# VectorE 32x32 blocks and spread SBUF-to-SBUF transfers in place of some TensorE transposes in a one-layer hybrid decoder

## Chip, core and metric

One core of one Trainium2 chip runs the whole program. The metric is the device time of one execution in microseconds (us), lower is better. The engines are called PE (TensorE; PEld is its weight load), DVE (VectorE), ACT (ScalarE), POOL (GpSimd) and SP (SyncE, which here only issues transfers).

## What is computed

One decoder layer on 256 tokens of width 2048 in float32, and a final norm. Cut to what matters:

```python
h = rms_norm(x); z = h @ w_in                  # 2048 -> 10240
qa, ka, va, qb, kb, vb, ga, gb = split_columns(z)
oa = differential_attention(rope(qa), rope(ka), va)    # 8 heads
ob = stick_breaking_attention(qb, kb, vb)              # 8 heads
m  = sigmoid(ga) * (oa @ w_proj_a) + sigmoid(gb) * (ob @ w_proj_b)
x  = x + m @ w_out
x  = x + memory_cross_attention(rms_norm(x), rms_norm(mem))
u  = rms_norm(x) @ w_up                        # 2048 -> 11264
u  = causal_depthwise_conv(u)                  # width 3, along the tokens
x  = x + (silu(u[:, :5632]) * u[:, 5632:]) @ w_down
return rms_norm(x)
```

## The kernel before

Every matrix product is cut into units of 512 output columns. `product` (L177) keeps two PSUM tiles of 128 tokens x 512 columns for a unit and walks over the contraction in 128-row blocks. Weights arrive by SP in 1 MB pieces (four 128-row blocks, tile `raw`, three buffers). `split_w` (L160) divides each half of a piece, 128 x 1024 values, into a high part on ACT (L162) and a low part on DVE (L163), in three buffers each; `mm3` (L166) then issues three matmuls per block and token half: high x high (L168), low x high (L169), high x low (L170). A unit over 2048 rows is four pieces, eight halves and 96 matmuls of 512 columns.

Products need the activations with the features on the partitions, while a unit's result has the tokens there. So results are transposed in 128 x 128 squares on PE, against an identity, into PSUM: `transposed` (L113, matmul L134) for the merge `mT`, the residuals `x1T`, `x2T` and the cross-attention inputs; `proj_T` (L243, matmul L258) for the queries and keys of both attentions; `gated` (L555, matmul L562) for each of the 22 units of the up projection. One unit is 8 squares. The copy out of PSUM is ACT and DVE work (L117, L118, L122, L123, L260), or the convolution itself, whose ACT (L568) and DVE instructions (L570, L572) read the transposed PSUM tile.

This side work is written as generators. `spawn(gen, delay)` starts one after so many halves, `tick` runs after each half of a product and lets the due ones go on; a `yield n` asks for n more halves. A scheduler then fixes the order of each engine's instructions, apart from SP's, which keeps the order of the program text. An SP instruction that must wait holds up all later transfers, the weights among them.

The up projection's loop (L585) evacuates both PSUM tiles of a unit to `zu` with the scale `r2` (L588) and spawns `gated` two halves later. The SBUF tiles that live long (`x2T`, `xr`, `gT`, queries, keys, gates) share one pool of 34 buffers, `b4`.

Of the kernel before, what the change touches and what calls it, by code (L numbers as in the profile page):

```python
# [17 lines left out]
S = 256          # tokens  # L18
NT = S // P      # token blocks
D = 2048  # L20
KD = D // P      # 128-row blocks of the model width
FF = 5632
KF = FF // P
U = 512          # columns of one product unit
KB = 4           # 128-row blocks per weight transfer
# [6 lines left out]
# columns of the packed per-partition parameters  # L32
# [13 lines left out]
def hybrid_layer(ctx: ExitStack, tc: tile.TileContext, x, xT, mem, memT, gmix, par, gfin,  # L46
# [28 lines left out]
    # additive masks of the diagonal blocks: [q, k] -> 0 where k <= q (k < q), else NEG  # L75
# [8 lines left out]
    # Work that is emitted between the products: generators that yield the number of  # L84
    # half blocks of weights to let pass before they go on.
# [6 lines left out]
    def tick(most=2):  # L92
        clock[0] += 1
        for t in [t for t in tasks if t[0] <= clock[0]][:most]:
            try:
                t[0] = clock[0] + next(t[1])
            except StopIteration:
                tasks.remove(t)
# [14 lines left out]
    def split(dst, src, gains=None):  # L113
        """dst[:, 0] + dst[:, 1] = src, or src * gain, in two parts of 12 bits.
        dst [P, 2, 2, S], src [P, 2, S]; gains: a [P, 1] column per 128-row block."""
# [10 lines left out]

    def transposed(dst, src, n, name, gains=None):
        """dst: act tiles of the 4 row blocks n*4.. of the transpose; src [P, NT, U]."""
# [11 lines left out]

    def sumsq(dst, src):
        junk = wk.tile([P, U], F32, tag="w2", name="junk")
        nc.scalar.activation(out=junk[:, :src.shape[-1]], in_=src, func=AF.Square, accum_out=dst)

    def rstd(ss, n, width, name):
        """(sum over the last axis of ss [P, n, m] / width + EPS) ** -0.5 -> [P, n]"""
# [19 lines left out]
    def mm3(out, a, b, start=True, stop=True):  # L166
        """out (+)= (a[0] + a[1]).T @ (b[0] + b[1]) without the product of the two low parts."""
# [9 lines left out]
    def product(xs, w, u, kt_n, name, pieces=None, before=None, heap=False):  # L177
        """x @ w[:, unit u] for both token blocks -> two PSUM tiles [P, U].
        pieces: 128-row blocks per transfer; before(kt): called ahead of the transfer from kt on."""
# [25 lines left out]
    def load_split(src, gains, i, name):  # L205
        """Split act tile i of a transposed input [P, KD, S] in DRAM, scaled by gains."""
# [27 lines left out]
    def proj_T2(ps, r, name):  # L234
        """Evacuate a unit scaled by r and transpose it: act tiles of heads 0, 1 and 2, 3."""
# [7 lines left out]
    def proj_T(ps, r, name, rotate=False):  # L243
        """Evacuate a unit scaled by r and transpose it: [P (dim), 4 (head), S]."""
# [9 lines left out]
        def rest():  # L254
            for t in range(NT):
                pt = sm_tile(f"{name}_tp")
                for h in range(4):
                    nc.tensor.transpose(out=pt[:, h * P:(h + 1) * P],  # L258
                                        in_=zs[t][:, h * P:(h + 1) * P], identity=ident)
                nc.vector.tensor_copy(out=dst[:, :, t * P:(t + 1) * P],  # L260
                                      in_=pt.rearrange("p (h s) -> p h s", h=4))
            yield 0
        spawn(rest(), 2)
        return dst

    def proj_n(ps, r, name):
        """Evacuate a unit scaled by r: [P (token), NT, U]."""
# [5 lines left out]
    def attn_T(a, name):  # L273
        """Causal weights of one head [q block][P, K] -> [P (key), 3 * P]:
        keys 0 for both query blocks, then keys 1 for query block 1."""
# [8 lines left out]
    # differential attention  # L284
    oaT = [None] * 4

    def diff_head(h):
        qT, kT, v, hh = qa[h // 4], ka[h // 4], va[h // 4], h % 4
        # scores of the two maps, in a bank each: query block 0 in 0:P, query block 1 in P:3 * P
# [62 lines left out]
    # stick-breaking attention, two heads at a time  # L352
    obT = [None] * 4

    def stick_pair(g):
        aw = [[], []]
        for i in range(NT):
# [14 lines left out]
            # softplus(z) = max(z, 0) + ln(1 + exp(-|z|)), zero where masked  # L372
# [27 lines left out]
    # the input projection in units; the attention of a group of heads runs between the products  # L400
# [21 lines left out]
    # lam = exp(q1.k1) - exp(q2.k2) + LAM_INIT, negated, on all partitions  # L422
# [19 lines left out]
    for i in range(2):  # L442
# [3 lines left out]
        spawn(chain(diff_head, (4 * i, 4 * i + 2)))  # L446
        spawn(chain(diff_head, (4 * i + 1, 4 * i + 3)), 2)
    for i in range(2):
# [3 lines left out]
        spawn(chain(stick_pair, (2 * i, 2 * i + 1)))  # L452
# [3 lines left out]
    # branch projections, gated and merged  # L456
    mT = [None] * 8
    for n in range(4):
# [9 lines left out]
        spawn(transposed(mT, ga, n, f"mT{n}"), 2)  # L468
# [6 lines left out]
    # output projection and residual  # L475
# [14 lines left out]
    for n in range(4):  # L490
# [4 lines left out]
        spawn(transposed(x1T, xr[n], n, f"x1T{n}", lambda k: col("g_x", k)), 2)  # L495
# [57 lines left out]
    gT = [None] * (KF // 2)  # L553

    def gated(i, z):  # L555
        us = []
        for part in range(2):          # gate, value
            pt = sm_tile("uT").rearrange("p (j s) -> p j s", j=2)
            for j in range(2):
                for t in range(NT):  # L560
                    c = (2 * part + j) * P
# [22 lines left out]
    for i in range(KF // 2):  # L584
        ps = product(x2T, w_up, i, KD, f"up{i}")  # L585
        z = [wk.tile([P, U], F32, tag="w2", name=f"zu{t}") for t in range(NT)]
        for t in range(NT):
            nc.scalar.activation(out=z[t], in_=ps[t], func=AF.Copy, scale=r2[:, t:t + 1])  # L588
# [123 lines left out]
```

## Time and profile before

| | |
|---|---|
| median of 3 runs | 1521.09 us (1521.03 to 1521.51) |
| profiled execution, from its first to its last instruction | 1518.9 us; its own time outside that span is not listed, the runs' median is 2.2 us above it |
| PE busy | 1503.4 us, 99% of the span, 6904 matmuls |
| PEld, DVE, ACT, POOL busy | 82%, 59%, 52%, 4% |
| clock that PE was granted | mean 0.998 of full speed |
| transfers | 287.78 MB, 189 GB/s, 54.5% of the 16 DMA engines' time on SP's queue |

The page gives the busy time of each engine, then the same in 40 slices of the span, then the transfers, and then the chain of work that ended last. A busy PE row is made of pipelined matmuls, so starts in the timeline say more than durations.

### The profile page before, as it was taken

The numbers are of one execution on the slowest core, as the hardware profiler recorded it, in microseconds if no ns is written. First come the engines' busy times: TensorE is split into PE (matmuls) and PEld (weight loads), VectorE is DVE, ScalarE is ACT, GpSimd is POOL, SyncE is SP. The second block draws the span as 40 slices with busy tenths as digits, with TensorE's granted clock in tenths as the row PEclk, the third lists the DMA queues.
The fourth block names the chain that finished last, engine by engine and source line by source line (L and its number), as shares of the span: only waits on it lengthen the run. The fifth ranks groups of instructions, "written<-read, shape, count | busy, mean of one in ns | idle before, by whom it ended". The sixth has DMA issues, their size and how long they took to land.

```text
span 1518.9 us, 17599 instructions
## 1 busy us (share of the span) xinstructions
PE 1503.4 (99%) x6904; PEld 1243.2 (82%) x6904; DVE 896.7 (59%) x1131; ACT 784.7 (52%) x1074; POOL 53.7 (4%) x72
## 2 busy tenths in 40 slices
PE   8999999999999999999999999999999999999997
PEld 6878788888888888888888888888888888888886
DVE  5575666564444565664666667666666666444562
ACT  6454555465555344664565555555555555344441
POOL 0202000000000010000000000000000000000010
PEclk9999999999999999999999999999999999999999
DMA  9544444445555556755355555555555555655561
GB/s 349 187 159 152 162 166 167 167 166 194 194 194 193 183 193 246 265 197 192 139 191 174 189 194 178 183 194 185 179 191 192 174 190 192 222 194 192 197 230 73
DMA packets 44003, 287.78 MB, mean 189 GB/s; under 512 B 5008, under 2 KB 5008, under 8 KB 11152
## 3 DMA queue, kind: packets, MB, share of 16 engines
q1 hardware_dynamic: 43488, 286.13, 54.5%
q8 instruction: 54, 0.88, 0.2%
q10 hardware_dynamic: 432, 0.53, 0.1%
q14 instruction: 29, 0.24, 0.0%
HBM read 284.54 MB, written 2.10 MB: 189 GB/s over the span
## 4 chain that ended last, share of the span: by engine, by line
PE 98%; issue 1%; DMA 0%; DVE 0%; ACT 0%; SPq 0%; POOLq 0%; POOL 0%; DVEq 0%
PE up_mm L170 11%; PE up_mm L169 11%; PE up_mm L168 11%; PE dn_mm L168 5%; PE dn_mm L170 5%; PE dn_mm L169 5%; PE g_mm L168 4%; PE g_mm L169 4%; PE g_mm L170 4%; PE wo_mm L170 2%; PE wo_mm L168 2%; PE wo_mm L169 2%; PE uT L562 1%; PE va_mm L169 1%; PE qb_mm L169 1%; PE qb_mm L168 1%
## 5 line engine op out<-in xcount | busy, mean ns | idle before, releaser
L163 DVE TENSOR_TENSOR up_lo<-up_raw,up_hi 128x1024 fp32r<-128x1024 f32 x176 | 215.7, 1226 | 170.3 <-ACT up_hi L162 167.8
L162 ACT CAST up_hi<-up_raw 128x1024 fp32r<-128x1024 f32 x176 | 185.5, 1054 | 197.5 <-PE up_mm L170 176.5
L170 PE MATMUL up_mm<-up_hi,x2T 128*128 128x512 f32 x704 | 274.1, 389 | 0.0
L169 PE MATMUL up_mm<-up_lo,x2T 128*128 128x512 f32 x704 | 274.0, 389 | 0.0
L168 PE MATMUL up_mm<-up_hi,x2T 128*128 128x512 f32 x704 | 254.8, 392 | 0.0
L163 DVE TENSOR_TENSOR dn_lo<-dn_raw,dn_hi 128x1024 fp32r<-128x1024 f32 x88 | 109.9, 1253 | 101.0 <-ACT dn_hi L162 95.7
L170 PEld LDWEIGHTS up_mm<-up_hi,x2T 128*128 128x128 f32 x704 | 132.2, 188 | 27.4
L169 PEld LDWEIGHTS up_mm<-up_lo,x2T 128*128 128x128 f32 x704 | 132.3, 188 | 26.7
L168 PEld LDWEIGHTS up_mm<-up_hi,x2T 128*128 128x128 f32 x704 | 132.2, 188 | 26.6
L162 ACT CAST dn_hi<-dn_raw 128x1024 fp32r<-128x1024 f32 x88 | 92.0, 1056 | 118.0 <-PE dn_mm L170 103.7
L170 PE MATMUL dn_mm<-dn_hi,gT 128*128 128x512 f32 x352 | 136.9, 389 | 0.0
L169 PE MATMUL dn_mm<-dn_lo,gT 128*128 128x512 f32 x352 | 136.9, 389 | 0.0
L163 DVE TENSOR_TENSOR g_lo<-g_raw,g_hi 128x1024 fp32r<-128x1024 f32 x64 | 78.4, 1225 | 83.8 <-ACT g_hi L162 83.8
L168 PE MATMUL dn_mm<-dn_hi,gT 128*128 128x512 f32 x352 | 126.3, 389 | 0.0
L162 ACT CAST g_hi<-g_raw 128x1024 fp32r<-128x1024 f32 x64 | 67.3, 1053 | 73.4 <-PE g_mm L170 70.2
L169 PE MATMUL g_mm<-g_lo,hT 128*128 128x512 f32 x256 | 100.0, 391 | 0.0
L170 PE MATMUL g_mm<-g_hi,hT 128*128 128x512 f32 x256 | 99.8, 390 | 0.0
L168 PE MATMUL g_mm<-g_hi,hT 128*128 128x512 f32 x256 | 90.7, 391 | 0.0
L170 PEld LDWEIGHTS dn_mm<-dn_hi,gT 128*128 128x128 f32 x352 | 66.1, 188 | 13.8
L169 PEld LDWEIGHTS dn_mm<-dn_lo,gT 128*128 128x128 f32 x352 | 66.1, 188 | 13.7
L168 PEld LDWEIGHTS dn_mm<-dn_hi,gT 128*128 128x128 f32 x352 | 66.1, 188 | 13.6
L170 PEld LDWEIGHTS g_mm<-g_hi,hT 128*128 128x128 f32 x256 | 48.1, 188 | 10.0
(301 smaller groups left out, 2664.5 us busy)
## 6 DMA issues: line engine op xcount, KB each, us to landing
up_raw<-in_w_up SPq DMA_DIRECT2D x88, 1024.0 KB, 4.9
dn_raw<-in_w_dn SPq DMA_DIRECT2D x44, 1024.0 KB, 4.9
g_raw<-in_w_in SPq DMA_DIRECT2D x32, 1024.0 KB, 5.0
wo_raw<-in_w_out SPq DMA_DIRECT2D x16, 1024.0 KB, 5.0
ka_raw<-in_w_in SPq DMA_DIRECT2D x8, 1024.0 KB, 6.1
va_raw<-in_w_in SPq DMA_DIRECT2D x8, 1024.0 KB, 5.0
qb_raw<-in_w_in SPq DMA_DIRECT2D x8, 1024.0 KB, 4.9
kb_raw<-in_w_in SPq DMA_DIRECT2D x8, 1024.0 KB, 4.9
```

What stands on the lines that cost most here:

```text
L162: nc.scalar.copy(out=hi, in_=src)
L163: nc.vector.tensor_tensor(out=lo, in0=src, in1=hi.bitcast(F32), op=ALU.subtract)
L168: nc.tensor.matmul(out, lhsT=a[0], rhs=b[0], start=start, stop=False)
L169: nc.tensor.matmul(out, lhsT=a[0], rhs=b[1], start=False, stop=False)
L170: nc.tensor.matmul(out, lhsT=a[1], rhs=b[0], start=False, stop=stop)
L562: nc.tensor.transpose(out=pt[:, j, t * P:(t + 1) * P], in_=z[t][:, c:c + P], identity=ident)
```

## The change

A new helper `turn` transposes the 32 x 32 blocks of a 128 x 512 tile on DVE; `regroup` then moves the blocks to their places with 16 SBUF-to-SBUF transfers on SP, each from 32 partitions to 32 partitions in 256 runs of 128 bytes, two transfers per half of a product. `flipped` does this for the merge units 0 and 1 and the first residual's units 0 to 2; `proj_T` does it for all eight units of queries and keys; the up projection does it for all 22 units, where ACT now scales the PSUM tiles in place. `transposed` on PE stays for the rest. Delays of the attention chains and of `gated` grow, and `tick` lets four tasks go on instead of two. Comments were removed, so line numbers shift (L162 is L195 now, L163 is L196, L562 is gone).

```diff
-    def tick(most=2):
+    def tick(most=4):
...
+    def turn(blk, src, t):
+        nc.vector.transpose(out=blk[:, :, t * P:(t + 1) * P], in_=src.rearrange("p (f c) -> p f c", c=P))
+
+    def regroup(dst, blk, per=2):
+        q = P // 4
+        d, s = (v.rearrange("p f (t c) -> p (f t) c", t=NT) for v in (dst, blk))
+        for i in range(16):
+            a, b = i // 4, i % 4
+            nc.sync.dma_start(out=d[b * q:(b + 1) * q, :, a * q:(a + 1) * q],
+                              in_=s[a * q:(a + 1) * q, :, b * q:(b + 1) * q])
+            if i % per == per - 1:
+                yield 1
+
+    def flip_tile(name):
+        return chunk_tile(f"{name}_blk", [P, U // P, S])
...
+    def flipped(dst, src, n, name, gains=None):
+        blk = flip_tile(name)
+        for t in range(NT):
+            turn(blk, src[:, t], t)
+        yield 8
+        z = chunk_tile(f"{name}_z", [P, U // P, S])
+        yield from regroup(z, blk)
+        for h in range(2):
+            k0 = 4 * n + 2 * h
+            dst[k0 // 2] = act_tile(f"{name}_{h}")
+            split(dst[k0 // 2], z[:, 2 * h:2 * h + 2], None if gains is None else [gains(k0), gains(k0 + 1)])
+        yield 0
...
         def rest():
+            blk = flip_tile(name)
             for t in range(NT):
-                pt = sm_tile(f"{name}_tp")
-                for h in range(4):
-                    nc.tensor.transpose(out=pt[:, h * P:(h + 1) * P],
-                                        in_=zs[t][:, h * P:(h + 1) * P], identity=ident)
-                nc.vector.tensor_copy(out=dst[:, :, t * P:(t + 1) * P],
-                                      in_=pt.rearrange("p (h s) -> p h s", h=4))
-            yield 0
-        spawn(rest(), 2)
+                turn(blk, zs[t], t)
+            yield 7
+            yield from regroup(dst, blk)
+        spawn(rest(), 1)
...
-        spawn(chain(diff_head, (4 * i, 4 * i + 2)))
-        spawn(chain(diff_head, (4 * i + 1, 4 * i + 3)), 2)
+        spawn(chain(diff_head, (4 * i, 4 * i + 2)), 10)
+        spawn(chain(diff_head, (4 * i + 1, 4 * i + 3)), 12)
...
-        spawn(chain(stick_pair, (2 * i, 2 * i + 1)))
+        spawn(chain(stick_pair, (2 * i, 2 * i + 1)), 10)
...
-        spawn(transposed(mT, ga, n, f"mT{n}"), 2)
+        spawn((flipped if n < 2 else transposed)(mT, ga, n, f"mT{n}"), 0 if n < 2 else 2)
...
-        spawn(transposed(x1T, xr[n], n, f"x1T{n}", lambda k: col("g_x", k)), 2)
+        spawn((flipped if n < 3 else transposed)(x1T, xr[n], n, f"x1T{n}", lambda k: col("g_x", k)), 0 if n < 3 else 2)
...
-    def gated(i, z):
+    def gated(i, blk):
+        uT = chunk_tile("uT", [P, U // P, S])
+        yield from regroup(uT, blk)
         us = []
-        for part in range(2):          # gate, value
-            pt = sm_tile("uT").rearrange("p (j s) -> p j s", j=2)
-            for j in range(2):
-                for t in range(NT):
-                    c = (2 * part + j) * P
-                    nc.tensor.transpose(out=pt[:, j, t * P:(t + 1) * P], in_=z[t][:, c:c + P],
-                                        identity=ident)
+        for part in range(2):
             u = wk.tile([P, 2, S], F32, tag="w2", name="u")
             for j in range(2):
                 f = part * KF + 2 * i + j
+                z = uT[:, 2 * part + j]
...
-        z = [wk.tile([P, U], F32, tag="w2", name=f"zu{t}") for t in range(NT)]
-        for t in range(NT):
-            nc.scalar.activation(out=z[t], in_=ps[t], func=AF.Copy, scale=r2[:, t:t + 1])
-        spawn(gated(i, z), 2)
+        blk = flip_tile(f"up{i}")
+        for t in range(NT):
+            nc.scalar.activation(out=ps[t], in_=ps[t], func=AF.Copy, scale=r2[:, t:t + 1])
+            turn(blk, ps[t], t)
+        spawn(gated(i, blk), 8)
```

What this does to the order on the engines is shown at three places. The first is SP in the middle of the up projection; `up_raw` is a weight piece, `uT` the transposed unit, `up_blk` the unit with its blocks turned, and the names in brackets are the eight completion semaphores of transfers (DMAHW0 to 7) and the engines that an issue waits for. Before:

```order
L190 DMA up_raw<-in_w_up 128x2048 [waits DMAHW1_49,DVE_49]
L190 DMA up_raw<-in_w_up 128x2048 [waits DMAHW2_49,DVE_49]
L190 DMA up_raw<-in_w_up 128x2048 [waits DMAHW3_49,DVE_49]
L190 DMA up_raw<-in_w_up 128x2048 [waits DMAHW4_49,DVE_49]
L190 DMA up_raw<-in_w_up 128x2048 [waits DMAHW5_49,DVE_49]
```

With the change:

```order
L223 DMA up_raw<-in_w_up 128x2048 [waits DMAHW4_49,DVE_49]
L138 DMA uT<-up_blk 32x8x32 [waits DMAHW5_49]
L138 DMA uT<-up_blk 32x8x32 [waits DMAHW6_49]
L138 DMA uT<-up_blk 32x8x32 [waits DMAHW7_49,PE_49]
L138 DMA uT<-up_blk 32x8x32 [waits DMAHW0_49]
L223 DMA up_raw<-in_w_up 128x2048 [waits DMAHW1_49,DVE_49]
L138 DMA uT<-up_blk 32x8x32 [waits DMAHW2_49]
L138 DMA uT<-up_blk 32x8x32 [waits DMAHW3_49]
L138 DMA uT<-up_blk 32x8x32 [waits DMAHW4_49]
```

Four small transfers stand behind each weight piece, and each issue waits for the transfer eight places before it, which used the same semaphore.

The second place is ACT from the end of one unit of the up projection to the end of the next. The casts to `up_hi` are the high parts of coming halves, the ACTIVATE on `u` is the convolution's first step, `sg` the sigmoid, the cast to `gT` the end of a unit's side work. Before:

```order
L588 ACTIVATE zu_6550<-up_mm_6381,r_6044 128x512
L588 ACTIVATE zu_6551<-up_mm_6382,r_6044 128x512
L162 CAST up_hi<-up_raw 128x1024 x3
L568 ACTIVATE u<-uT,pc 128x256 x2
L162 CAST up_hi<-up_raw 128x1024
L568 ACTIVATE u<-uT,pc 128x256 x2
L162 CAST up_hi<-up_raw 128x1024
L576 ACTIVATE sg<-u 128x512
L162 CAST up_hi<-up_raw 128x1024
L117 CAST gT_6618<-sg 128x512
L162 CAST up_hi<-up_raw 128x1024 x2
L588 ACTIVATE zu_6723<-up_mm_6554,r_6044 128x512
```

With the change:

```order
L615 ACTIVATE up_mm_6823<-up_mm_6823,r_6150 128x512
L615 ACTIVATE up_mm_6824<-up_mm_6824,r_6150 128x512
L195 CAST up_hi<-up_raw 128x1024 x6
L595 ACTIVATE u<-uT,pc 128x256 x4
L195 CAST up_hi<-up_raw 128x1024
L603 ACTIVATE sg<-u 128x512
L195 CAST up_hi<-up_raw 128x1024
L117 CAST gT_7174<-sg 128x512
L615 ACTIVATE up_mm_7004<-up_mm_7004,r_6150 128x512
L615 ACTIVATE up_mm_7005<-up_mm_7005,r_6150 128x512
```

The convolution's ACT steps have moved to the end of the unit in one lump, and the cast to `gT` now stands directly ahead of the next evacuation.

The third place is SP in the mixer, where the queries and keys of the first group are regrouped at the same time (`qaT`, `kaT`). Before, only weight pieces stood there:

```order
L190 DMA qa_raw<-in_w_in 128x2048 [waits DMAHW7_49,DMAHW4_49,DVE_49]
L190 DMA qa_raw<-in_w_in 128x2048 [waits DMAHW5_49,DVE_49]
L190 DMA qa_raw<-in_w_in 128x2048 [waits DMAHW6_49,DMAHW1_49,DVE_49]
L190 DMA qa_raw<-in_w_in 128x2048 [waits DMAHW7_49,DVE_49]
L190 DMA ka_raw<-in_w_in 128x2048 [waits DMAHW0_49,DVE_49]
```

With the change, from one weight piece to the next:

```order
L223 DMA qa_raw<-in_w_in 128x2048 [waits DMAHW4_49,DVE_49]
L138 DMA qaT_495<-qaT_blk 32x8x32 [waits DMAHW5_49]
L138 DMA qaT_495<-qaT_blk 32x8x32 [waits DMAHW6_49]
L138 DMA kaT_512<-kaT_blk 32x8x32 [waits DMAHW7_49]
L138 DMA kaT_512<-kaT_blk 32x8x32 [waits DMAHW0_49]
L138 DMA qaT_495<-qaT_blk 32x8x32 [waits DMAHW1_49]
L138 DMA qaT_495<-qaT_blk 32x8x32 [waits DMAHW2_49]
L138 DMA kaT_512<-kaT_blk 32x8x32 [waits DMAHW3_49]
L138 DMA kaT_512<-kaT_blk 32x8x32 [waits DMAHW4_49]
L223 DMA qa_raw<-in_w_in 128x2048 [waits DMAHW5_49,DVE_49]
```

Eight small transfers stand between two weight pieces here, and the last of them waits for the piece ahead of them.

## Rows read from the trace of the kernel before

**Rows 1.** The page: busy time, slices of PE, granted clock, and the chain by engine

```profile
span 1518.9 us, 17599 instructions
PE 1503.4 (99%) x6904; PEld 1243.2 (82%) x6904; DVE 896.7 (59%) x1131; ACT 784.7 (52%) x1074; POOL 53.7 (4%) x72
PE   8999999999999999999999999999999999999997
PEclk9999999999999999999999999999999999999999
PE 98%; issue 1%; DMA 0%; DVE 0%; ACT 0%; SPq 0%; POOLq 0%; POOL 0%; DVEq 0%
```

**Rows 2.** The chain, 798 to 802 us: start, us, what

```profile
799.10 0.23 PE up_mm L170
799.33 0.87 PE uT L562 x8
```

**Rows 3.** Transposing matmuls by tile: duration ns min/median/max, first and last start

```profile
L562 PE MATMUL uT<-ident,zu x176: 270/272/273, 799.2 to 1275.6; 128*128 128x128 f32 x176
...
L258 PE MATMUL qaT_tp<-ident,qaT_z x16: 270/272/273, 49.9 to 128.7; 128*128 128x128 f32 x16
...
L134 PE MATMUL mT_tp<-ident,gate x32: 271/272/273, 517.4 to 587.5; 128*128 128x128 f32 x32
...
L134 PE MATMUL x1T_tp<-ident,xr x32: 270/272/273, 607.8 to 676.6; 128*128 128x128 f32 x32
```

**Rows 4.** ACT timeline, evacuations of two units that follow each other: start, us

```profile
815.89 1.37 ACT L588 ACTIVATE zu<-up_mm,r 128x512 f32<-128x512 f32 x2 [0.93 <-PE up_mm L170]
...
838.55 1.37 ACT L588 ACTIVATE zu<-up_mm,r 128x512 f32<-128x512 f32 x2 [0.93 <-PE up_mm L170]
```

**Rows 5.** Windows, up projection, mixer, output projection: us, busy by engine, clock, DMA share, GB/s

```profile
798.90:1276.60 477.70, 477.70 (x2198) 397.60 (x2197) 311.35 (x401) 268.06 (x340) 0.00 (x0) 1.00 0.54 185
...
42.00:304.00 262.00, 262.00 (x1256) 212.53 (x1255) 162.37 (x267) 130.81 (x231) 23.91 (x41) 1.00 0.48 165
...
574.00:664.00 90.00, 90.00 (x414) 74.76 (x413) 56.41 (x70) 53.81 (x89) 3.54 (x2) 1.00 0.71 251
```

**Rows 6.** DMA view, 2 to 4 us, then 1513.5 to 1518.9 us: ACT's queue

```profile
q10 hardware_dynamic: 144, 0.01, 4.8%
...
q10 hardware_dynamic: 144, 0.26, 13.7%
```

**Rows 7.** SP timeline: two issues

```profile
4.98 1.34 SPq L418 DMA_DIRECT2D pc<-in_par  x1
...
15.25 0.33 SPq L215 DMA_DIRECT2D r_c<-in_x  x1
```

**Rows 8.** Waits of SP's queue, and issues with median us to landing

```profile
SPq L190 <- DVE up_lo L163: 464.3, 88, 6.0
...
up_raw<-in_w_up SPq DMA_DIRECT2D x88, 1024.0 KB, 4.9
ka_raw<-in_w_in SPq DMA_DIRECT2D x8, 1024.0 KB, 6.1
...
out<-xr SPq DMA_DIRECT2D x6, 256.0 KB, 2.3
```

**Rows 9.** Groups of DVE and ACT instructions: busy us, mean ns, idle before

```profile
L163 DVE TENSOR_TENSOR up_lo<-up_raw,up_hi 128x1024 fp32r<-128x1024 f32 x176 | 215.7, 1226 | 170.3 <-ACT up_hi L162 167.8
L162 ACT CAST up_hi<-up_raw 128x1024 fp32r<-128x1024 f32 x176 | 185.5, 1054 | 197.5 <-PE up_mm L170 176.5
...
L578 DVE TENSOR_TENSOR sg<-u,sg 128x512 f32<-128x512 f32 x22 | 15.2, 692 | 0.8
L117 ACT CAST gT<-sg 128x512 fp32r<-128x512 f32 x22 | 13.7, 625 | 0.5 <-DVE sg L578 0.5
...
L260 DVE COPY qbT<-qbT_tp 128x512 f32<-128x512 f32 x4 | 2.7, 686 | 2.0 <-PE qbT_tp L258 2.0
...
L377 DVE TENSOR_TENSOR_SCAN cb<-ones,lb 128x256 f32<-128x256 f32 x4 | 2.5, 678 | 0.1
```

More of the change, by code (lines that the diff above doesn't have):

```diff
@@ L566, in gated @@
                 f = part * KF + 2 * i + j
+                z = uT[:, 2 * part + j]
                 tap = lambda k: col("cw", k * 2 * KF + f)
-                nc.scalar.activation(out=u[:, j], in_=pt[:, j], func=AF.Identity, scale=tap(2),
+                nc.scalar.activation(out=u[:, j], in_=z, func=AF.Identity, scale=tap(2),
                                      bias=col("cb", f))
-                nc.vector.scalar_tensor_tensor(out=u[:, j, 1:], in0=pt[:, j, 0:S - 1], scalar=tap(1),
+                nc.vector.scalar_tensor_tensor(out=u[:, j, 1:], in0=z[:, 0:S - 1], scalar=tap(1),
                                                in1=u[:, j, 1:], op0=ALU.mult, op1=ALU.add)
-                nc.vector.scalar_tensor_tensor(out=u[:, j, 2:], in0=pt[:, j, 0:S - 2], scalar=tap(0),
+                nc.vector.scalar_tensor_tensor(out=u[:, j, 2:], in0=z[:, 0:S - 2], scalar=tap(0),
                                                in1=u[:, j, 2:], op0=ALU.mult, op1=ALU.add)
```

## Prediction

> **What bounds the kernel now.** I read the page first, then the chain of waits, then the windows by stage. The page shows one engine that never rests: PE is busy for 99% of the span, at 9 or more tenths in all but the first and last slices, at full clock, and the chain that ended last runs through PE for 98% of its length [rows 1]. So a microsecond taken off PE is a microsecond off the program, as long as the weights and their split parts still arrive in time. The chain through the up projection shows what the change takes away: matmul after matmul at 0.23 us, and in between one block of eight transposes that holds the chain for 0.87 us [rows 2]. The transposes are not hidden behind anything: PE is in order, and the next matmul starts when the block is over. Two evacuations that follow each other are 838.55 - 815.89 = 22.66 us apart, the period of one unit [rows 4]. Without its block it would be 21.79 us.
>
> **What is removed.** Transposes for 35 units leave PE: 176 on `uT` (22 units of 8), 4 x 16 on queries and keys (8 units), half of the 32 on `mT` (2 units) and 24 of the 32 on `x1T` (3 units) [rows 3], in all 280, or 35 blocks of eight. The same duration, 0.27 us, in every one of these rows lets me price every block like the one on the chain. 35 x 0.87 = 30.5 us leave PE's path.
>
> **What is added to DVE and ACT.** Each unit gets two `turn`s of 128 x 512. No 32 x 32 transpose is in the trace, so I bound it: the nearest row of its shape is the copy of 128 x 512 out of PSUM at 0.69 us, the dearest per column the scan at 0.68 us for 256 columns, which makes 1.36 us for 512 [rows 9]. I take 0.69, because a transpose also reads and writes each value once, and keep 1.36 for the range. For queries and keys the `turn` takes the place of just such a copy. In the up projection DVE is busy for 311.35 of 477.70 us, 14.8 us per unit [rows 5]; with two more instructions that is 16.2 us of 21.79, at the dear end 17.5. ACT stays near 268.06 / 477.70 x 22.66 = 12.7 us. Neither becomes the bound by its sum; their order is a rival below. The Trainium skill (VectorE: DVE Perf Modes, section on the three transpose paths) gives 311 ns for a VectorE transpose of 128 x 128 in bf16; four of them would be an estimated 1.24 us, and nothing here shows it.
>
> **What is added to the DMA engines.** A unit is regrouped by 16 transfers of 256 runs of 128 bytes. A transfer also sends 16 completions, as the 144 packets for 128 rows show [rows 6]. So each of the 16 engines gets 16 x 272 / 16 = 272 small packets per unit. From 2 to 4 us ACT's queue carried only `gm`, rows of 64 bytes: 4.8% of 16 engines over 2 us is 1.54 us for 144 packets, 10.7 ns each. At the end it carried rows of 2048 bytes: 13.7% over 5.4 us is 11.8 us, 91 ns a row once the completions are taken off [rows 6]. 128 bytes lie next to the first of these; on the line between them a packet costs 13.3 ns, and 272 cost 3.6 us. The weights take 0.54 of the DMA engines' time [rows 5], 12.2 us of a 22.66 us unit. 12.2 + 3.6 = 15.8 us fit into 21.79 us. The transfers fill the engines only from (21.79 - 12.2) / 272 = 35 ns a packet on. The bounds are 10.7 and 91 ns.
>
> **What is added on SP.** An issue cost 0.33 us for 144 packets and at most 1.34 us, while the engines were full at the start [rows 7]. A unit of the up projection now has 4 weight pieces and 16 small transfers: 20 x 0.33 = 6.6 us, at worst 4 x 0.33 + 16 x 1.34 = 22.8 us. The first fits easily; the second would pace the unit 0.1 us above today's and is another thing that ends the gain, at 1521 + 22 x 0.1 - 13 x 0.87 = 1512; I count its chance with that of the late third half. I take 0.33. What SP does with its time today is wait: 464.3 us in the up projection for a weight buffer, 88 times [rows 8]. A small transfer that waits there for its `turn` delays the next piece, which now lands 4.9 us after its issue [rows 8]. Three buffers are ahead of PE by two pieces, 2 x 5.4 = 10.9 us, so some 6 us of delay are covered. The `turn` is done about 4 us after its unit ends, while the regroup was spawned eight halves later and SP runs two pieces ahead of PE, so it asks for it about then. That wait costs nothing while the cover lasts.
>
> **The sum.** 1518.9 - 30.5 = 1488.4 us for the span; the median of the runs is 2.2 us above the span of the profile, so 1490.6, and I say 1491.
>
> **Rivals.**
>
> *The third half comes late, 1507 us.* Against the gain speaks the new ACT order: the cast to `gT` stands directly ahead of the evacuation. It waits for two DVE products, which stand behind the low part of the next unit's second half. That low part is done about when the unit ends, since the cast before it waits for PE to free a buffer. Then come 2 x 0.69, the cast 0.62, two evacuations 1.37 [rows 4, 9], the high part 1.05 and the low part 1.23 us [rows 9]: 5.65 us. PE needs the third half's low part 2 x 2.72 us after the unit's end and two matmuls more, at 5.9. So by my sum it holds with 0.25 us to spare, where the old order, evacuation first, had 2 us. If a `turn` costs 1.36, the second one ends at 5.4 us and the low part at 6.65: 0.75 us late per unit, 22 x 0.75 = 16.5 us. Anything that makes the convolution's transfers late comes out in the same place. It decides from a `turn` of 0.98 us on.
>
> *The DMA engines fill up, slower, about 1670 us.* No row of before shows a transfer from SBUF to SBUF. From 38 ns a packet ((22.66 - 12.2) / 272) a unit takes longer than today. Halfway from there to the 91 ns of a 2 KB row, at 65 ns, it takes 12.2 + 17.6 = 29.8 us; 22 x 7.1 - 13 x 0.87 = +146 us. For it speaks only that such packets have not been seen; against it, that 64 bytes cost 10.7 ns and not 91, so a packet is paid mostly by its bytes [rows 6]. The Trainium skill (VectorE: DVE Perf Modes, the three transpose paths) speaks for it: it warns of a plain DMA that transposes by strides, 19 times slower than the crossbar's 1309 ns for 128 x 128 in bf16. For the eight squares of a unit that is an estimated 199 us, and a program of several milliseconds. Here DVE has turned the blocks before, so that 128 bytes stay together; whether the warning holds for such runs no row tells.
>
> *The eight places, 1496 us.* In the mixer eight small transfers stand between two pieces, and the last of them waits for the piece ahead, which landed in 4.9 to 6.1 us [rows 8]. A piece then takes up to 6.1 + 0.7 us instead of 5.4: four pieces lose up to 5.4 us. I expect the cover of 6 us to hold, as DMA is at 0.48 there, against 0.71 in the output projection, where the three residual units add to the loads [rows 5].
>
> *Nothing changes.* The freed time of PE could come back as waits for split halves, at 1521. Against it: DVE waits today for ACT 167.8 us and is not late itself [rows 9].
>
> **How the numbers follow.** My forecast has 0.70, the late third half 0.14, the full DMA engines 0.08, the eight places 0.04, nothing 0.04. Faster by more than 0.2%, about what a measurement can tell here, is the first, second and fourth: 0.88; within it 0.04; slower 0.08. The range goes from 1486, where a block is worth 1.0 us and not 0.87, to 1508, which takes in the late third half; 0.88 of the chance lies in it, and 0.74 would without it.
>
> **What would show it.** Right: no `uT` matmuls, evacuations 21.8 us apart, weights still ahead (no wait of PE for `up_hi` or `up_lo`), a `turn` near 0.69 us, small packets near 13 ns and the DMA share in the up projection near 15.8 / 21.8 = 0.73. Wrong: PE idle before the third half of each unit (the order), a DMA share near 1 with late landings (the packets), or SP issues well above 0.33 us and PE waiting for `qa_hi` around 80 us (the queue).

## The result, and the profile after

The changed kernel is slower: 1556.99 us (1555.25 to 1564.64, 4 runs) against 1521.06 us (1520.54 to 1521.51, 4 runs), a ratio of 1.0247 with a 95% interval of 1.0221 to 1.0273. The forecast was 1491 us, and the range ended at 1508.

The page of the changed kernel, with the lines that answer to [rows 1, 8, 9]; the last one is from its list of transfers (issues, KB each, median us to landing):

```profile
span 1554.2 us, 17855 instructions
PE 1489.5 (96%) x6624; PEld 1217.4 (78%) x6624; DVE 929.1 (60%) x1185; ACT 789.5 (51%) x1080; POOL 51.9 (3%) x72
q1 hardware_dynamic: 195808, 304.51, 62.1%
PE 90%; ACT 3%; DVE 3%; DMA 2%; issue 1%; SPq 0%; POOLq 0%; POOL 0%; DVEq 0%; ACTq 0%
L129 DVE STREAM_TRANSPOSE up_blk<-up_mm 128x512 f32<-128x512 f32 x44 | 30.6, 717 | 53.8 <-ACT up_mm L615 53.8
uT<-up_blk SPq DMA_DIRECT2D x352, 32.0 KB, 4.6
```

All 280 transposes are gone (6904 matmuls became 6624), a `turn` costs 0.717 us, a small transfer lands in 4.6 us, and the DMA engines are far from full. But PE is down from 99% to 96%, and ACT, DVE and DMA have entered the chain: PE waits now, and the profile must say where. The view by tile (duration ns min/median/max, first to last start) places the loss by the gate product `g_mm` and the up product `up_mm`. Before:

```profile
L168 PE MATMUL g_mm<-g_hi,hT x256: 387/389/580, 310.0 to 489.0; 128*128 128x512 f32 x128
L168 PE MATMUL up_mm<-up_hi,x2T x704: 387/389/482, 770.9 to 1268.8; 128*128 128x512 f32 x176
```

After:

```profile
L201 PE MATMUL g_mm<-g_hi,hT x256: 387/389/580, 322.9 to 505.4; 128*128 128x512 f32 x128
L201 PE MATMUL up_mm<-up_hi,x2T x704: 387/389/628, 783.0 to 1303.3; 128*128 128x512 f32 x176
```

So the stretch to the first gate matmul took 12.9 us more, the gate units 182.5 - 179.0 = 3.5 us more, the stretch from there to the up projection 281.9 - 277.6 = 4.3 us less (five blocks of 0.87 us, as forecast), and the up projection 520.3 - 497.9 = 22.4 us more, where 21 x 0.87 = 18.3 us less was forecast (the block of the last unit comes after the last product, so 21 of the 22 lie in this stretch). Two places lost, one kept its promise.

**The up projection.** The chain of the changed kernel from the end of a unit to the first matmuls of the next (start, us, what):

```profile
870.57 0.66 ACT up_mm L615
...
871.83 1.04 ACT up_hi L195
...
872.90 1.24 DVE up_lo L196
```

PE's unit is over, and the next unit's first matmul has no weights: ACT evacuates first and casts the first half afterwards. PE's timeline at the same place:

```profile
870.82 0.39 PE L203 MATMUL up_mm<-up_hi,x2T 128*128 128x512 f32 x1
872.92 0.73 PE L201 MATMUL up_mm<-up_hi,x2T 128*128 128x512 f32 x2 [1.71 <-ACT up_hi L195]
874.18 0.50 PE L202 MATMUL up_mm<-up_lo,x2T 128*128 128x512 f32 x1 [0.53 <-DVE up_lo L196]
```

Three matmuls take 874.18 - 870.82 = 3.36 us, where three starts are 0.68 us apart elsewhere: 2.68 us lost. The same pair of stops stands at 15 of the 22 unit ends, 14 of them inside the up projection: 14 x 2.68 = 37.5 of the 22.4 + 18.3 = 40.7 us that are missing there. Matmuls at a lower clock add 1.6 us behind the first of these stops (last section); the other 1.6 us are not assigned. ACT's timeline ahead of the stop shows that nothing made ACT late:

```profile
863.09 1.06 ACT L195 CAST up_hi<-up_raw 128x1024 fp32r<-128x1024 f32 x1
866.76 0.62 ACT L117 CAST gT<-sg 128x512 fp32r<-128x512 f32 x1 [2.62 <-DVE sg L605]
870.57 1.34 ACT L615 ACTIVATE up_mm<-up_mm,r 128x512 f32<-128x512 f32 x2 [3.18 <-PE up_mm L203]
871.83 2.93 ACT L195 CAST up_hi<-up_raw 128x1024 fp32r<-128x1024 f32 x3
```

For 3.18 us ACT stood idle, waiting for PE to end the unit, with a cast behind the evacuation that could have run (experiment 1 runs it there). Its weights were there; the SP timeline:

```profile
854.54 0.33 SPq L223 DMA_DIRECT2D up_raw<-in_w_up  x1
...
859.99 0.33 SPq L223 DMA_DIRECT2D up_raw<-in_w_up  x1
860.37 2.56 SPq L138 DMA_DIRECT2D uT<-up_blk  x4
```

The piece of the late casts is the one issued at 854.54 us, and pieces land 5.4 us after their issue. It is the order on ACT. The 2% of DMA in the page's chain do not speak against it: at three of these stops (unit ends at 896.77, 992.29 and 1087.89 us) the chain names the landing of a small transfer, but the first cast starts 1.26 us after the evacuation there, as it does at 870.57. Counted through its instructions in issue order, two casts of the next unit stand ahead of the evacuation in all 22 units before; after the change the counts by unit are 2 2 2 0 0 0 2 0 0 0 2 0 0 0 2 0 0 0 2 0 0 0. The 15 zeros are the 15 stops.

**The mixer.** The chain of the changed kernel at its first large stop:

```profile
123.52 0.86 PE sa L325 x8
...
124.84 0.26 DVE o L367
...
125.24 0.51 PE oaT L372 x2
...
127.33 0.93 ACT pa L337 x4
...
129.17 0.43 DVE pa L345
...
129.64 0.47 PE da_tp L307
```

Scores, `oaT` and the next transposes of attention weights follow each other on PE without a product matmul between them, so each waits for the norm or softmax of the one before. The casts for the next product (`va`) stand on ACT behind these exponentials and the evacuation, at 129.27 us. Their weights were there, and SP was waiting for a buffer and not the other way round (SP's timeline):

```profile
115.78 0.33 SPq L223 DMA_DIRECT2D va_raw<-in_w_in  x1
...
133.91 0.33 SPq L223 DMA_DIRECT2D va_raw<-in_w_in  x1
```

The same happens at 207 us (`kb`), and a similar lump of the stick-breaking attention stands at 290 us.

### The profile page after: what moved, and what is told of

The parts are those of the page before. It is cut to its first block, busy times and chain, and to the rows that moved or that the text cites. A ratio compares the mean times of both kernels' runs of the same rounds, so it can differ in the third digit from the quotient of the medians.

```text
span 1554.2 us, 17855 instructions
## 1 busy us (share of the span) xinstructions
PE 1489.5 (96%) x6624; PEld 1217.4 (78%) x6624; DVE 929.1 (60%) x1185; ACT 789.5 (51%) x1080; POOL 51.9 (3%) x72
## 4 chain that ended last, share of the span: by engine, by line
PE 90%; ACT 3%; DVE 3%; DMA 2%; issue 1%; SPq 0%; POOLq 0%; POOL 0%; DVEq 0%; ACTq 0%
PE up_mm L202 9%; PE up_mm L203 9%; PE up_mm L201 9%; PE dn_mm L202 5%; PE dn_mm L203 5%; PE dn_mm L201 5%; PE g_mm L202 4%; PE g_mm L203 4%; PE g_mm L201 3%; PE wo_mm L202 2%; PE wo_mm L203 2%; PE wo_mm L201 2%; DVE up_lo L196 2%; DMA uT<-up_blk 1%; ACT up_hi L195 1%
## 5 line engine op out<-in xcount | busy, mean ns | idle before, releaser
L196 DVE TENSOR_TENSOR up_lo<-up_raw,up_hi 128x1024 fp32r<-128x1024 f32 x176 | 213.0, 1223 | 110.3 <-ACT up_hi L195 95.0
L203 PE MATMUL up_mm<-up_hi,x2T 128*128 128x512 f32 x704 | 274.8, 390 | 0.0
L201 PE MATMUL up_mm<-up_hi,x2T 128*128 128x512 f32 x704 | 248.4, 393 | 24.0 <-ACT up_hi L195 24.0
L195 ACT CAST up_hi<-up_raw 128x1024 fp32r<-128x1024 f32 x176 | 181.7, 1049 | 137.3 <-PE up_mm L203 128.9
L196 DVE TENSOR_TENSOR dn_lo<-dn_raw,dn_hi 128x1024 fp32r<-128x1024 f32 x88 | 109.7, 1253 | 91.5 <-ACT dn_hi L195 86.4
L202 PEld LDWEIGHTS up_mm<-up_lo,x2T 128*128 128x128 f32 x704 | 132.4, 188 | 40.8 <-DVE up_lo L196 13.7
L195 ACT CAST dn_hi<-dn_raw 128x1024 fp32r<-128x1024 f32 x88 | 91.6, 1054 | 111.1 <-PE dn_mm L203 100.3
L196 DVE TENSOR_TENSOR g_lo<-g_raw,g_hi 128x1024 fp32r<-128x1024 f32 x64 | 78.3, 1225 | 85.9 <-ACT g_hi L195 85.8
L195 ACT CAST g_hi<-g_raw 128x1024 fp32r<-128x1024 f32 x64 | 66.9, 1050 | 66.4 <-PE g_mm L203 62.6
L129 DVE STREAM_TRANSPOSE up_blk<-up_mm 128x512 f32<-128x512 f32 x44 | 30.6, 717 | 53.8 <-ACT up_mm L615 53.8
```

Of the source, the lines that this page charges most:

```text
L129: nc.vector.transpose(out=blk[:, :, t * P:(t + 1) * P], in_=src.rearrange("p (f c) -> p f c", c=P))
L195: nc.scalar.copy(out=hi, in_=src)
L196: nc.vector.tensor_tensor(out=lo, in0=src, in1=hi.bitcast(F32), op=ALU.subtract)
L201: nc.tensor.matmul(out, lhsT=a[0], rhs=b[0], start=start, stop=False)
L202: nc.tensor.matmul(out, lhsT=a[0], rhs=b[1], start=False, stop=False)
L203: nc.tensor.matmul(out, lhsT=a[1], rhs=b[0], start=False, stop=stop)
```

## Experiments

Theory A: the scheduler's new order on ACT (and PE, in the mixer) lets PE run dry. Theory B: the small transfers hold the work up, through SP's queue or the DMA engines.

**1. Two casts ahead again, up projection only.** Evacuation and turn come two halves later, issued on ACT behind the cast that was written last (`cast[0]`, noted in `split_w`):

```diff
+        cast[0] = nc.cur_bb.bb.instructions[-1]
...
-        for t in range(NT):
-            nc.scalar.activation(out=ps[t], in_=ps[t], func=AF.Copy, scale=r2[:, t:t + 1])
-            turn(blk, ps[t], t)
-        spawn(gated(i, blk), 8)
+        def leave(i=i, ps=ps, blk=blk):
+            with tc.issue_after(cast[0]):
+                for t in range(NT):
+                    nc.scalar.activation(out=ps[t], in_=ps[t], func=AF.Copy, scale=r2[:, t:t + 1])
+            for t in range(NT):
+                turn(blk, ps[t], t)
+            yield 6
+            yield from gated(i, blk)
+        spawn(leave(), 2)
```

> The changed kernel with one thing altered: in the up projection the two evacuations of a unit (and so its two turns) are queued on ACT behind the first two casts of the next unit, in all 22 units, as they stand in the kernel before. The turns, the 352 small transfers, their places in SP's queue and the DMA work stay. Theory A (the order on ACT): in the changed kernel 15 units have no cast of the next unit ahead of the evacuation, and PE stands still for 0.92 + 2.10 - 2 x 0.23 = 2.57 us in each; 15 x 2.57 = 38.6 us, and 4.8 us of matmuls at the low clock behind such gaps, come back: 1557 - 43 = 1514 us (1510 to 1519). Theory B (the small transfers hold the unit up, by SP's queue or the DMA engines): their number and places are the same, so the time stays between 1550 and 1560 us.

Measured: 1513.07 us (1512.64 to 1513.98), ratio to before 0.9949 (0.9934 to 0.9964). Theory A. ACT's timeline now shows two casts in the wait for the unit's end:

```profile
867.85 0.62 ACT L118 CAST gT<-sg 128x512 fp32r<-128x512 f32 x1 [2.62 <-DVE sg L607]
868.38 1.04 ACT L196 CAST up_hi<-up_raw 128x1024 fp32r<-128x1024 f32 x1
869.67 1.05 ACT L196 CAST up_hi<-up_raw 128x1024 fp32r<-128x1024 f32 x1 [0.25 <-PE up_mm L205]
871.66 1.34 ACT L619 ACTIVATE up_mm<-up_mm,r 128x512 f32<-128x512 f32 x2 [0.93 <-PE up_mm L205]
```

The cast to `gT` waits as long for DVE as in the changed kernel (2.62 us); it was never what hurt. The 43 us were forecast with 4.8 us of them for matmuls at the low clock; the traces show it behind one unit end, at 1.6 us, while each stop with the slow starts behind it cost 2.8 us and not 2.57.

**2. The converse: the kernel before with no cast ahead,** in the same 15 units.

```diff
-        nc.scalar.copy(out=hi, in_=src)
+        if hold:
+            with tc.issue_after(hold.pop()):
+                nc.scalar.copy(out=hi, in_=src)
+        else:
+            nc.scalar.copy(out=hi, in_=src)
...
+        if i > 2 and i % 4 != 2:
+            hold.append(nc.cur_bb.bb.instructions[-1])
```

> The kernel before with one thing altered: in the same 15 units of the up projection as in the changed kernel, the next unit's first cast is queued on ACT behind the evacuations. No turn, no small transfer, all transposes on PE as before. Theory A (the order on ACT): PE stands still for about 2.57 us in each of 15 units, and some matmuls run at the low clock behind the gaps: 1521 + 38.6 + up to 5 = 1560 to 1565 us. Theory B (the small transfers): nothing that it blames is in this kernel, so 1521 us, and up to 1530 if the order costs a little.

Measured: 1548.91 us (1548.08 to 1549.01), ratio 1.0183 (1.0167 to 1.0198). With no turn and no small transfer, the order alone costs 27.8 us, 1.85 at each of the 15 places; theory B's 1521 to 1530 is out. Theory A's 1560 to 1565 is missed by 11 us, 0.7 a place, and PE's timeline says why: the eight transposes of the unit that has just ended fall into the stop and fill part of it.

```profile
862.45 0.44 PE L567 MATMUL uT<-ident,zu 128*128 128x128 f32 x2
863.13 0.87 PE L567 MATMUL uT<-ident,zu 128*128 128x128 f32 x6 [0.24 <-ACT zu L593]
864.06 0.73 PE L173 MATMUL up_mm<-up_hi,x2T 128*128 128x512 f32 x2
```

**3. The mixer's part alone, on the kernel before.** `proj_T`, the delays 10 and 12 and `tick(most=4)` as changed, all else as before.

> The kernel before with the mixer's part of the change alone: queries and keys turned and regrouped, attention chains 10 and 12 halves later, up to 4 tasks per half; merge, first residual and up projection as before. In the traces the stretch from the first attention work to the first gate matmul is 12.9 us longer after the change and the gate units 3.4 us. If the parts are independent: 1521 + 16.3 = 1537 us (1533 to 1541). If the mixer lost its time only through what the other parts do to the shared queues and pools: 1521 - 8 x 0.87 = 1514 us.

Measured: 1537.21 us (1537.02 to 1537.87), ratio 1.0108 (1.0091 to 1.0125). The mixer loses its time without the other parts. It does not say by which means.

**4. Up projection mended, mixer as before.** Experiment 1 with the old `proj_T` and the old delays.

> The kernel with two casts ahead of each evacuation in the up projection, and with the mixer as it was before (queries and keys transposed on PE, attention chains not delayed; still up to 4 tasks per half). Theory A (order): 27 blocks of transposes are gone and nothing waits, 1521 - 27 x 0.87 = 1497.5 us (1494 to 1502). Theory B (small transfers): the up projection still holds PE up, so above 1521 us.

Measured: 1496.48 us (1495.97 to 1496.78), ratio 0.9839 (0.9824 to 0.9853). 27 blocks gave 24.6 us, forecast 23.5. With the 16.1 us of experiment 3 this makes 1521.1 - 24.6 + 16.1 = 1512.6, and experiment 1, which has both, took 1513.07: the parts are independent. The window of its up projection (us; busy PE, PEld, DVE, ACT, POOL; clock, DMA share, GB/s) beside [rows 5]:

```profile
768.00:1247.00 479.00, 479.00 (x2119) 396.68 (x2118) 347.15 (x449) 276.46 (x351) 0.69 (x1) 1.00 0.73 216
```

**5 and 6. The mixer, by the same means,** on experiment 1. In 5 the evacuations of queries and keys come two halves later behind a cast (the edit of experiment 1, made in `proj_T`); 6 is 5 with the regrouping started two halves sooner.

```diff
-            yield 6
+            yield 4
             yield from regroup(dst, blk)
```

> The kernel with two casts ahead in the up projection, and in the mixer too: the evacuation and turn of each query and key unit come two halves later and behind a cast of the next unit (2 or 3 casts ahead at the first two of the places where PE stood still, where the changed program had none). The order of the attention pieces on PE stays close to the changed program's: at both places scores, oaT and the first transpose of the weights stand with at most two product matmuls between them. Theory A1 (PE stands still in the mixer because these pieces follow each other directly, each waiting for the softmax or norm of the one before): the pieces are still together, so most of the 16 us stay lost: 1505 to 1514 us. Theory A2 (only the missing casts): the gaps at these two places go, 1496 to 1503 us. Theory B (the small transfers of queries and keys are late): 1513 us.

Measured: 1510.21 us (1507.97 to 1510.28), ratio 0.9927 (0.9912 to 0.9942). Most of the loss stays while the attention pieces stay together, as A1 said; A2 is out. B's 1513 is only 3 us off, so this run does not part A1 from B.

> As the run with the evacuations behind casts in the mixer, and the regrouping starts two halves sooner after the turn. In the order of PE that comes out, 23 product matmuls stand between scores and oaT and 23 more ahead of the next transposes of weights at the first place, 15 and 32 at the second. Theory A1 (attention pieces back to back on PE): the gaps of 5 us at these two places and the slow matmuls behind them are gone, 1513 - 8 to 16 = 1497 to 1505 us; with all of the mixer's loss undone and its 8 blocks gained it would be 1489.5 us. Theory B (the small transfers are late): starting them sooner ahead of their turns can only hold SP longer, 1513 us or more.

Measured: 1523.14 us (1521.71 to 1525.21, 10 runs), ratio 1.0017 (1.0007 to 1.0027). A1's figure was missed by 18 us although the pieces are apart, and here the small transfers do hold the weights up. SP's timeline:

```profile
123.79 1.25 SPq L141 DMA_DIRECT2D qaT<-qaT_blk  x2
152.38 1.24 SPq L141 DMA_DIRECT2D kaT<-kaT_blk  x2
153.72 0.54 SPq L228 DMA_DIRECT2D va_raw<-in_w_in  x1
```

Asked for too early, the small transfer waits for its `turn`, which DVE reaches only at about 151.7 us behind the attention, and the next weight piece waits behind it on SP. This was the mechanism of my line on SP's cover of 6 us; in the changed kernel itself a small transfer made SP wait for 5.8 us at most, within the cover.

**7. The mixer's small transfers on ACT's queue,** on experiment 1.

```diff
-            nc.sync.dma_start(out=d[b * q:(b + 1) * q, :, a * q:(a + 1) * q],
+            (eng or nc.sync).dma_start(out=d[b * q:(b + 1) * q, :, a * q:(a + 1) * q],
...
-            yield from regroup(dst, blk)
+            yield from regroup(dst, blk, 2, nc.scalar)
```

> The kernel with two casts ahead in the up projection; in the mixer the 128 small transfers of queries and keys are issued from ACT's queue and no longer from SP's. In the order that comes out, 24 product matmuls stand between scores and oaT at the first place and the evacuations have 2 or 3 casts ahead. Theory A1: the gaps at the first two places shrink: 1497 to 1508 us, less what ACT pays for 128 issues (up to 128 x 0.62 = 79 us of ACT time beside PE's 245 us, ACT is busy 125 us there, so it should hide). Theory B (SP's queue is what delays the weights in the mixer on the chip): the loss of 16 us goes whole, 1490 to 1497 us.

Measured: 1489.74 us (1489.10 to 1490.08), ratio 0.9795 (0.9781 to 0.9810), the fastest kernel of the study. From its page:

```profile
PE 1470.9 (99%) x6624; PEld 1212.6 (82%) x6624; DVE 930.7 (63%) x1185; ACT 794.2 (53%) x1082; POOL 51.8 (3%) x72
PE 96%; ACT 2%; issue 1%; DVE 1%; DMA 1%; SPq 0%; ACTq 0%; POOLq 0%; POOL 0%; DVEq 0%
```

This fits B's figure better than A1's, but two things changed together: SP was freed, and the scheduler's order became another, with 24 product matmuls between scores and `oaT`. Experiment 8 takes the order back.

**8. The kernel of experiment 7 with the bad order at two places.** The transfers stay on ACT's queue; only the first cast behind `ka1` and behind `kb0` is held back, with the `hold` of experiment 2.

```diff
+            if name in ("kaT1", "kbT0"):
+                hold.append(nc.cur_bb.bb.instructions[-1])
```

> The fastest kernel so far (two casts ahead in the up projection, the mixer's small transfers on ACT's queue, 1489.7 us) with two instructions moved: the first cast of the next unit is queued behind the evacuation of the second key unit of each pair in question (the last key unit of the differential attention, the first of the stick-breaking one), as in the changed program. The order of PE that comes out has scores, oaT, transposes of weights, scores and transposes of weights again without a product matmul between them at the first place, and with two at the second, row by row like the changed program. The transfers stay on ACT's queue. Theory A1 (the order of PE and ACT makes the mixer's loss): PE stands still at these two places as after the change, 1.23 + 4.24 and 2.22 + 3.63 us less 0.2 each, and runs at half clock for some 4 us behind each (2 us more): 1489.7 + 12 to 16 = 1502 to 1506 us. Theory B (the small transfers in SP's queue make it): they are not in SP's queue, so 1490 to 1494 us.

Measured: 1505.34 us (1504.94 to 1506.21), ratio 0.9898 (0.9883 to 0.9912). Two casts, held back, cost 15.6 us with SP's queue free of small transfers: A1's range, and B's is out. At the first place the price is not a clean one, for the chain of this run has issues on ACT's queue in it, 2.9 of the 6.9 us from 122.59 us to the next transposes, where the changed kernel's chain has no transfer:

```profile
124.37 0.61 ACTq L140
...
125.00 0.63 ACTq L140
...
129.47 0.47 PE da_tp L316
```

The second place is clean: such issues take 0.2 us of its chain, and from the first to the last start of `qb_mm`, which takes it in, the times are 98.5 us in experiment 7, 106.7 here and 106.9 in the changed kernel. The mixer's whole loss is 1513.07 - 1489.74 = 23.3 us. The remaining 7.7 us lie in the stretch of the third lump: from the last start of `qb_mm` to the first of `g_mm` it is 50.7 us in experiment 7, 50.2 here and 58.9 in the changed kernel. What makes that lump was not tried by itself. Of theory B little is left in the mixer: PE never waited for a small transfer there in the changed kernel, and for 0.9, 0.6 and 1.6 us in all in experiments 1, 3 and 5.

**9 and 10. How far are the transfers from being the bound?** Both start from experiment 4. In 9 every small transfer of the up projection is issued twice.

> The kernel with two casts ahead in the up projection and the mixer as before (1496.5 us), with every small transfer of the up projection issued twice (704 in place of 352). It measures how far the transfers are from being the bound. By the rows of the mended run an issue takes SP about 0.62 us and 32 of them with 4 pieces 32 x 0.62 + 4 x 0.33 = 21.2 us of a unit of 21.8; the DMA engines would be at 0.54 x 22.66 + 2 x 3.7 = 19.6 us of 21.8. Theory A (the transfers cost nothing while they fit): 1496 to 1512 us, the upper end if the waits on transfers eight places back take what is left of SP's time. Theory B (each small transfer costs the unit time now): the up projection grows by at least as much again as it has lost, above 1530 us.

Measured: 2252.02 us (2249.62 to 2252.89), ratio 1.4806. Each copy writes the same place and so waits on SP for the landing of the first: 737.6 us of SP's waits, 353 times, are for `uT` transfers. It tells what waits for landings cost on an in-order queue (33.5 us a unit), and nothing of the issues, so it does not answer the question. In 10 the second transfer goes to a tile of its own.

```diff
+            if copy is not None:
+                c = copy.rearrange("p f (t c) -> p (f t) c", t=NT)
+                nc.sync.dma_start(out=c[b * q:(b + 1) * q, :, a * q:(a + 1) * q],
+                                  in_=s[a * q:(a + 1) * q, 0:2, b * q:(b + 1) * q])
```

> The kernel with two casts ahead in the up projection and the mixer as before (1496.5 us), with a second small transfer behind each of the 352 of the up projection, into a tile of its own that nothing reads, with a quarter of the bytes: twice the issues on SP without the wait of each copy for the first that made the run with every transfer issued twice 2252 us. An issue takes 0.64 us, so SP needs 32 x 0.64 + 4 x 0.33 = 21.8 us of a unit of 21.8; the DMA engines 0.73 x 21.8 + 0.25 x 3.7 = 16.8 us. Theory A (issues cost nothing while they fit): just at the edge, 1497 to 1515 us. Theory B (each small transfer already costs time): 1530 us or more.

Measured: 1567.08 us (1565.46 to 1568.58), ratio 1.0299 (1.0282 to 1.0316), 52 us past theory A's upper end. SP's timeline, from one weight piece to the next:

```profile
1005.20 0.53 SPq L229 DMA_DIRECT2D up_raw<-in_w_up  x1
1005.77 0.59 SPq L139 DMA_DIRECT2D uT<-up_blk  x1
1006.41 0.61 SPq L143 DMA_DIRECT2D spare<-up_blk  x1
...
1009.65 0.59 SPq L139 DMA_DIRECT2D uT<-up_blk  x1
1010.56 0.59 SPq L143 DMA_DIRECT2D spare<-up_blk  x1
1011.25 0.53 SPq L229 DMA_DIRECT2D up_raw<-in_w_up  x1
```

SP rests only for the 0.3 us in which the last of the eight waits for the piece eight places back. From the first to the last product the up projection takes 1310.5 - 768.0 = 542.5 us, 24.7 a unit or 6.2 a piece: SP's own pace. The DMA engines are not the bound, at 0.67 of their time from 800 to 1300 us. In experiment 4 the units take 21.8 us, PE's own pace. So there is a cliff; 16 transfers a unit are this side of it, 32 beyond, and theory B would hold there.

**11. All small transfers on ACT's queue** (`nc.scalar` for `nc.sync` in `regroup`), on the changed kernel, nothing held back by hand.

> The changed kernel with all small transfers issued from ACT's queue in place of SP's, and nothing else altered: no instruction is held back by hand. The order that comes out has two casts ahead of the evacuation in all 22 units of the up projection by itself. Theory A (the order on ACT and PE made the loss, and the planner's order goes wrong when the small transfers fill SP's queue in its plan): no gaps of 2.1 and 0.92 us behind the evacuations; ACT then carries 276.8 / 22 + 16 x 0.62 = 22.5 us a unit, 0.7 us more than PE's 21.8, so 1490 to 1507 us, and somewhat more if casts stand behind issues. Theory B (the small transfers themselves): no better than 1545 us.

Measured: 1519.61 us (1514.21 to 1526.77, 10 runs), ratio 1.0000 (0.9983 to 1.0017). The stops behind the evacuations are gone, 37 us against the changed kernel, and the upper figure of A is still missed by 12.6 us. Two casts stand ahead of the evacuation in all 22 units of the trace (the fastest of the ten runs), but the up projection takes 500.1 us from first to last start, against 520.3 in the changed kernel and 479.0 in experiment 4: PE still waits 11.4 us for split weights, now inside the units. ACT's timeline shows the new wait:

```profile
996.95 1.05 ACT L195 CAST up_hi<-up_raw 128x1024 fp32r<-128x1024 f32 x1 [2.34 <-DMA uT<-up_blk]
1001.46 2.08 ACT L595 ACTIVATE u<-uT,pc 128x256 f32<-128x256 f32 x4 [3.46 <-DMA uT<-up_blk]
1003.44 1.98 ACT L195 CAST up_hi<-up_raw 128x1024 fp32r<-128x1024 f32 x2
```

The convolution waits on ACT for transfers that ACT itself issued late, and casts stand behind it. In the mixer the same queue had room.

## Why the prediction was wrong, point by point

- **The block, right.** The 21 blocks in the up projection gave 497.9 - 479.0 = 18.9 us, 0.90 us each where I had 0.87, and the 35 blocks 1520.9 - 1489.7 = 31.2 us in experiment 7, where I had 30.5. My 1491 us is the time of this change with another order and with the mixer's transfers on ACT's queue.
- **`turn` and packets, right.** 0.717 us for the 0.69 taken; the estimate of 1.24 us beside it was too high. The DMA share of the mended up projection is 0.73, as forecast, so a small packet costs an estimated (0.73 x 21.8 - 12.2) / 272 = 13.7 ns, where 13.3 was the guess. The rival of the full DMA engines is out. The warning of the Trainium skill (VectorE: DVE Perf Modes, the three transpose paths), which the page gives for a large innermost stride of the destination, does not hold for these runs of 128 bytes: a unit's 16 transfers hide here beside 21.8 us of matmuls.
- **SP's issue, mis-sized without harm.** 0.64 us from one small issue to the next instead of 0.33: 16 x 0.64 + 4 x 0.33 = 11.6 us of SP a unit instead of 6.6. It fits into 21.8; twice as many did not. The rival priced from this term, 1512, was counted into the chance of the range, which ends at 1508.
- **The step that failed: "So by my sum it holds with 0.25 us to spare".** The place was the right one, the order around the evacuation on ACT. The sum said "PE needs the third half's low part", that is, two casts of the next unit stand ahead of the evacuation. That was true of the rows before. In the rows after, which stood on record next to it, no cast stands between the cast to `gT` and the evacuation, and the sum holds only if the two casts around the sigmoid are the next unit's. The eight casts between the two evacuations fit that reading too. Only a count from the first unit on tells: in the trace six casts ahead of the convolution's steps and two behind them, as in those rows, stand between two unit ends that both have the count 0 (896.77 and 921.34 us), and all eight belong to the unit that ends. So the first half, not the third, was the late one. With my own prices the first half's high part comes 1.37 + 1.05 = 2.4 us and its low part 3.7 us after the unit's end; PE stood for 2.7. At 15 units that is 40 us, more than the whole gain. The rival of the late third half (1507) had the place and the wrong half, and asked for a dearer `turn`, which never came.
- **The mixer, not looked at.** I read the third place on SP only. The attention chains were moved 10 and 12 halves, and what that does to PE's and ACT's order there stood in the sum at nothing, without a reason. Its lumps cost 23 us, where 7 were to be gained and the rival of the eight places was priced at 5.4.
- **The cover on SP, right for the changed kernel, wrong as a freedom.** Experiment 6 shows the price as soon as a transfer is asked for ahead of its `turn`.

Why the scheduler chose these orders is only partly settled. With the small transfers off SP and nothing else altered, two casts stand ahead in all 22 units and the stops behind the evacuations are gone (experiment 11). That its plan takes SP for fuller than the trace shows it is a guess that no run tests.

## What to carry to other kernels

When a change adds work to a queue that a scheduler plans around, compare the new order in every unit, not at one place: count how many of the next unit's preparations stand ahead of each instruction that waits for the end of this one. A gain of 0.87 us a unit is gone if one cast of 1.05 us falls on the wrong side of such a wait, whatever the busy shares say. Pinning the evacuations behind two casts by hand brought 44 us here, more than the 31 us of the idea itself.

## What the runs showed of the hardware

A stop of PE can cost more than its length. The windows of the changed kernel at the mixer's first stop (as above: busy, then clock, DMA share, GB/s):

```profile
126.00:130.00 4.00, 0.36 (x1) 0.18 (x1) 2.92 (x10) 3.73 (x12) 1.04 (x3) 0.67 0.00 0
130.00:134.00 4.00, 4.00 (x16) 2.91 (x16) 3.56 (x5) 2.22 (x3) 3.77 (x6) 0.50 0.01 2
```

PE had stood for 3.91 us, waiting for the softmax; it was then granted 0.50, the 1.2 GHz level, over the 4 us in which it worked again; in experiment 7, without the stop, the granted clock of the same stretch is 1.00. But not every stop does this. The 4 us behind the first two of the 15 unit ends at which PE stops in the up projection:

```profile
874.17:878.17 4.00, 3.99 (x11) 3.15 (x12) 2.23 (x2) 0.59 (x1) 0.00 (x0) 0.59 0.46 123
900.37:904.37 4.00, 3.99 (x18) 3.30 (x18) 2.53 (x3) 1.65 (x2) 0.00 (x0) 1.00 0.46 123
```

PE stood for 1.71 and 0.53 us at both, and behind the other 13 the granted clock is 1.00 as well. The unit behind the first took 26.2 us and the next one 24.6. What made the first place differ the runs do not show.

An issue of a transfer of 32 partitions in 256 runs takes SP or ACT about 0.61 us, while a weight piece of 1 MB takes 0.33, or 0.53 when SP had no pause before it.
